# Two transformer blocks on one core: attention weights left undivided until after the values

## The chip, the core and the metric

The kernel runs on one core of a Trainium2 chip, in one launch. The time is that of the device, in microseconds (us), from the start to the end of the program; the median of a few runs is given. PE is the matrix engine, PEld its weight loads, DVE the vector engine, ACT the scalar engine, POOL the general one, SP the queue that issues most transfers. The matrix engine writes into PSUM, eight banks of 128 x 512 float32.

## The reference

512 latent tokens and 256 context tokens of width 1024 go through two blocks of two layers each, batch 1, all in float32.

- Block 1, each layer: a gated linear attention (4 heads), a sliding-window attention (6 query heads over 2 key heads, window 128, all 256 context keys, and a sink) and a neighbourhood attention (6 heads, 8 rows x 32 columns of keys with a learned bias, and the context keys), then an output projection and a SwiGLU. In the first layer the context tokens run through the same steps (there both attentions see the 256 context keys alone).
- Block 2, each layer: an attention over the 128 keys that an indexer selects (8 heads), whose output is normalised per head by its root mean square; an mLSTM beside it; output projection; SwiGLU.

What matters here is the softmax. With a sink it is

```
p = softmax(concat([s_loc, s_ctx, s_sink]))      # the sink is only in the sum
o = p_loc @ v_loc + p_ctx @ v_ctx
```

and without one the same without s_sink. In block 2 the output o then goes through `o * rsqrt(mean(o * o) + 1e-6) * w` per head of 64.

## The kernel before, in words

Activations lie with features on the 128 partitions and tokens along the free axis, weights are loaded in units of 128 x 1024 and split into two parts (`split`, L183), and each product of a projection is three matrix products of these parts (L147, L148, L150). PSUM's eight banks are dealt out as four pools: three for projections (`mm`), two for scores (`S`), two for transposes and broadcasts (`T`), one for attention outputs (`o`).

`attn_pair` (L341) does one block of 128 queries for two heads, whose features are the lower and upper 64 partitions. Scores go to an `S` bank for each head (L365, L369); DVE adds the negated bias or mask on the way to SBUF and keeps the running minimum (L377, two instructions, the second reads the minimum out); ACT takes the exponential with the row's sum (L382); DVE takes the reciprocal of that sum (L383) and multiplies the 128 x 512 or 128 x 640 weights by it (L384); PE transposes them (L392), ACT copies the first head's transposed weights to SBUF (L395), DVE the second's (L397); PE multiplies them with the values (L400) into the pair's `o` bank. For the sink, an extra column of the score buffer holds the negated sink (L357), so that the sum has it. The score buffers `sb` come from a pool of two in the latents' passes, three in the context's pass and four in block 2.

Three callers loop over pairs of heads and blocks of 128 queries. In `mixers` (block 1) they are three pairs of sliding-window heads, then three pairs of neighbourhood heads, each with four blocks for the latents and two for the context; after a pair the output is split from PSUM into two parts for the projection (L187 on ACT, L188 on DVE). In `mixers2` (block 2) the loop is over two halves of the tokens and four pairs, and after each pair the output is squared, normalised by `head_rms` and stored.

Between the blocks the code takes work from a queue of jobs (`tick`): projections of later pairs and output projections, as long as there are any. The Tile framework records all instructions, a list scheduler sets each engine's static order, and pools decide when a buffer comes free: an instruction that writes a buffer waits until the last reader of its former content is done.

Two helpers spread small columns over partitions. `bcast_rows` (L241) gives every partition a row of per-token factors by a matrix product of the broadcast column with the identity (L245), one for each 128 tokens. `head_rms` (L516) does so for the two halves apart (L527), two for each 128 tokens; it is called by the gated linear attention's output (`gla_out`) and by `mixers2`.

Of the kernel before, what the change touches and what calls it, by code (L numbers as in the profile page):

```python
# [10 lines left out]
F32 = mybir.dt.float32  # L11
# [40 lines left out]
class Kern:  # L52
# [90 lines left out]
    def gemm(self, out, terms):  # L143
        """out = the sum over terms (w_hi, w_lo, x_hi, x_lo) of w^T x; the low parts of w come last."""
# [33 lines left out]
    def side_banks(self):  # L178
        """banks that stand idle at the start of a phase"""
# [3 lines left out]
    def split(self, hi, lo, ps, scale=1.0):  # L183
        """hi + lo = scale * ps, hi rounded to float32r."""
# [9 lines left out]
    def rsqrt(self, pool, src, n, eps=EPS):  # L194
        V = self.nc.vector
        x, y, a, p = [self.til(pool, [P, 16], F32, f"rs{c}")[:, :n] for c in "xyap"]
        V.tensor_scalar(x, src, eps, None, op0=ALU.add)
# [13 lines left out]
    def sq_add(self, sg, k, x=None, pe=False):  # L211
        """pe: summed by the tensor engine, where the vector engine has enough to do"""
# [28 lines left out]
    def bcast_rows(self, r, n):  # L241
        """psum[p, 128 j + i] = r[i, j] for all p."""
        ps = self.bank(self.psT, "T")
        for j in range(n // P):
            self.nc.tensor.matmul(ps[:, j * P:(j + 1) * P], r[:, j:j + 1].to_broadcast([P, P]), self.ident, start=True, stop=True)  # L245
# [9 lines left out]
    def norm_seg(self, sg, a, b, h):  # L255
        """h = (x * rms) * a + b in two parts, of one segment."""
# [11 lines left out]
    def mod_units(self, wm, bm, cst, out, chunks, pool=None):  # L268
        """out[:, u, v] for chunks of 4 u; yields after each unit of two k-tiles.
        pool: for the raw weights, where nothing else wants the banks."""  # L270
# [37 lines left out]
    def mod_units_v(self, wm, bm, cv, out, chunks, pool, nv=lambda q: 1):  # L308
        """the same on the vector engine, for nv(q) of the vectors; yields after each unit."""
# [26 lines left out]
    def table(self):  # L336
        """exp and ln from one table set, from here on"""
        self.tc.keep_in_program_order(self.nc.scalar.preload_act_table_set("natural_log_exp_and_others"))

# [1 line left out]
    def attn_pair(self, heads, wide):  # L341
        """heads: dicts of q (hi, lo) or (plain, ), segs (k_hi, k_lo, n) along the keys, bias(c0, w): what is added to
        the negated scores (so that the running extreme is a minimum), init, sink, vs, o."""
# [10 lines left out]
        for x in heads:  # L354
            x["sb"], x["st"] = self.til(self.pb, [P, wide + 1], F32, "sb"), self.til(self.st, [P, 3], F32, "st")
            if x["sink"] is not None:
                V.tensor_copy(x["sb"][:, tot:tot + 1], x["sink"])  # L357
        for bi, (b0, w, idx) in enumerate(banks):
# [12 lines left out]
            for x, ps in zip(heads, pss):  # L371
# [5 lines left out]
                V.tensor_tensor_reduce(dst, src, bt, 1.0, x["init"], ALU.add, ALU.min, x["st"][:, bi:bi + 1])  # L377
                x["init"] = x["st"][:, bi:bi + 1]
        for x in heads:
            st, sb = x["st"], x["sb"][:, :tot]  # L380
            se = x["sb"][:, :tot + (x["sink"] is not None)]
            A.activation(se, se, AF.Exp, bias=x["init"], scale=-1.0, accum_out=st[:, 2:3])  # L382
            V.reciprocal(st[:, 2:3], st[:, 2:3])  # L383
            V.tensor_scalar(sb, sb, st[:, 2:3], None, op0=ALU.mult)  # L384
# [17 lines left out]
    def nat_gemm(self, units, h, toks, n, evac):  # L402
        """out[tok, n cols] for each 128 tokens; units: the k-tiles in equal parts, [P, per * n] each."""
# [75 lines left out]
    def gla_out(self, n, pair, v, dirs, gcol, sg, y):  # L479
        """dirs: per direction (q_in, k_in, states); y: (hi, lo) of [P, n]."""  # L480
# [35 lines left out]
    def head_rms(self, sq, n, rb=None):  # L516
        """1 / rms over each half of the partitions, broadcast back to [P, n] (in psum: rb)."""
# [5 lines left out]
        r = self.rsqrt(self.sm, ms[:, :2 * nt], 2 * nt)  # L523
        rb = self.bank(self.psS, "S") if rb is None else rb
        for j in range(nt):
            for i in range(2):
                nc.tensor.matmul(rb[64 * i:64 * i + 64, j * P:(j + 1) * P], r[:, 2 * j + i:2 * j + i + 1].to_broadcast([P, 64]),  # L527
                                 self.ident, start=True, stop=True)
        return rb

    def out_unit(self, src, u, per, ys, st, gcol, sg=None):
        """x += gcol * (w^T y) for columns [u * per, ...) of one unit [P, len(ys), per], of all tokens or of one segment."""
# [15 lines left out]
    def by_segs(self, segs, units, emit, cont, common=0):  # L548
        """emit(sgs, u): the first units of all segments together, the others segment by segment, and then
# [1253 lines left out]
```

## Time and profile before

| what | value |
|---|---|
| median of three runs | 3463.4 us (3456.02 to 3464.35) |
| profiled execution, its own time from first to last instruction | 3456.8 us |
| PE busy | 3340.1 us, 97%, 21110 instructions |
| DVE busy | 2104.6 us, 61%, 4540 instructions |
| ACT busy | 1322.4 us, 38%, 2322 instructions |
| POOL busy | 34.9 us, 1% |
| mean granted clock of PE | 0.974 |

The five attention stages lie at 115 to 225 us (context, first layer), 366 to 577 and 1330 to 1537 (latents, first and second layer), 2157 to 2275 and 2912 to 3037 (block 2). The busy time of PE contains the modelled tails of its matrix products, so a stretch with PE busy to 95% can still have waits in it; the starts of successive instructions tell more than their durations. "L400" is line 400 of the kernel, and an engine name in front says who executes it. [...]

### The profile page before, as it was taken

The page shows a single profiled execution, that of the slowest core. Times are in us where ns is not written, and L with a number is a line of the kernel's source. Part 1 is how long each engine was busy: PE and PEld are TensorE (multiplying, and loading weights), DVE is VectorE, ACT ScalarE, POOL GpSimd, SP SyncE. Part 2 cuts the span into 40 slices and gives each one's busy share as a digit, 9 for nine tenths or more (in the row PEclk, how much of TensorE's full clock was granted, in tenths as well). Part 3 has the DMA queues.
Part 4 walks back from the last instruction along what each step waited for, and adds up shares of the span by engine and source line. Part 5 has one row for each costly group of instructions (what it writes and reads, how often), then busy time and mean ns, then how long its engine had stood idle before and what let it go on. Part 6 is the DMA issues. An engine that isn't in the chain of part 4 may idle for free.

```text
span 3456.8 us, 53203 instructions
## 1 busy us (share of the span) xinstructions
PE 3340.1 (97%) x21110; PEld 2766.9 (80%) x21110; DVE 2104.6 (61%) x4540; ACT 1322.4 (38%) x2322; POOL 34.9 (1%) x62
## 2 busy tenths in 40 slices
PE   7999999999999999999999999999999999999999
PEld 5777667888889986678889977678889867688889
DVE  4656567645345856667665798565656797463335
ACT  4334244312122543443223474333224474343334
POOL 0000100000000000000000000000000000000000
PEclk9799999999999999999999999999999999899999
DMA  7353212324233421124664411145555211133335
GB/s 258 102 168 102 56 43 68 115 89 130 96 122 122 136 79 48 37 75 150 210 192 158 130 55 61 35 137 171 191 176 170 96 49 62 37 104 98 98 107 164
DMA packets 128768, 388.80 MB, mean 112 GB/s; under 512 B 27268, under 2 KB 32644, under 8 KB 128520
## 3 DMA queue, kind: packets, MB, share of 16 engines
q1 hardware_dynamic: 128520, 385.41, 34.8%
q8 instruction: 166, 2.72, 0.3%
q14 instruction: 82, 0.67, 0.1%
HBM read 383.25 MB, written 2.10 MB: 111 GB/s over the span
## 4 chain that ended last, share of the span: by engine, by line
PE 86%; DVE 7%; ACT 3%; DMA 2%; issue 2%; SPq 0%; DVEq 0%; ACTq 0%
PE mm L147 14%; PE mm L148 13%; PE mm L150 13%; PE mm L141 4%; PE mm L140 4%; PE mm L139 4%; PE o L400 3%; PE S L172 3%; PE mm L1288 3%; PE T L392 2%; PE S L369 2%; DVE wlo L188 1%; PE mm L172 1%; PE o L172 1%; PE S L365 1%
## 5 line engine op out<-in xcount | busy, mean ns | idle before, releaser
L188 DVE TENSOR_TENSOR wlo<-wraw,whi 128x1024 fp32r<-128x1024 f32 (+3 forms) x492 | 575.1, 1173 | 679.1 <-PE mm L150 397.2
L187 ACT CAST whi<-wraw 128x1024 fp32r<-128x1024 f32 (+3 forms) x492 | 494.9, 1010 | 874.4 <-PE mm L148 438.0
L147 PE MATMUL mm<-h_lat,whi 128*128 128x512 f32 x1816 | 722.0, 398 | 0.4 <-ACT whi L187 0.3
L148 PE MATMUL mm<-h_lat,whi 128*128 128x512 f32 x1816 | 716.7, 395 | 0.0
L150 PE MATMUL mm<-h_lat,wlo 128*128 128x512 f32 x1816 | 465.2, 393 | 0.0
L147 PEld LDWEIGHTS mm<-h_lat,whi 128*128 128x128 f32 x1816 | 342.0, 188 | 83.3 <-issue 6.8
L148 PEld LDWEIGHTS mm<-h_lat,whi 128*128 128x128 f32 x1816 | 342.2, 188 | 78.7 <-issue 11.7
L150 PEld LDWEIGHTS mm<-h_lat,wlo 128*128 128x128 f32 x1816 | 337.4, 188 | 75.3 <-issue 5.4
L325 DVE SCALAR_TENSOR_TENSOR macc<-mraw,cst,macc 128x512 f32<-128x512 f32 x280 | 207.1, 749 | 36.3 <-DMA mraw<-wm 32.3
L139 PE MATMUL mm<-ah,whi 128*128 128x256 f32 (+1 forms) x702 | 216.4, 308 | 1.2 <-DVE x_lat L1506 1.2
L140 PE MATMUL mm<-al,whi 128*128 128x256 f32 (+1 forms) x702 | 216.7, 309 | 0.0
L141 PE MATMUL mm<-ah,wlo 128*128 128x256 f32 (+1 forms) x702 | 216.7, 309 | 0.0
L382 ACT ACTIVATE sb<-sb,st 128x512 f32<-128x512 f32 (+6 forms) x184 | 119.7, 651 | 158.6 <-DVE st L377 125.9
L139 PEld LDWEIGHTS mm<-ah,whi 128*128 128x128 f32 x702 | 131.8, 188 | 9.0 <-ACT whi L187 1.4
L141 PEld LDWEIGHTS mm<-ah,wlo 128*128 128x128 f32 x702 | 131.8, 188 | 8.1
L140 PEld LDWEIGHTS mm<-al,whi 128*128 128x128 f32 x702 | 132.2, 188 | 7.4
L140 PE MATMUL mm<-b,whi 128*128 128x256 f32 (+1 forms) x462 | 136.9, 296 | 0.0
L139 PE MATMUL mm<-b,whi 128*128 128x256 f32 (+1 forms) x462 | 136.3, 295 | 0.0
L141 PE MATMUL mm<-b,wlo 128*128 128x256 f32 (+1 forms) x462 | 136.3, 295 | 0.0
L187 ACT CAST ah<-fx 128x256 fp32r<-128x256 f32 (+1 forms) x77 | 43.0, 559 | 199.9 <-DVE fx L876 199.9
L392 PE MATMUL T<-ident,sb 128*128 128x128 f32 x616 | 107.0, 294 | 9.0 <-DVE sb L384 3.6
L392 PEld LDWEIGHTS T<-ident,sb 128*128 128x128 f32 x616 | 73.1, 147 | 43.8 <-issue 16.5
(402 smaller groups left out, 6391.9 us busy)
## 6 DMA issues: line engine op xcount, KB each, us to landing
mraw<-wm SPq DMA_DIRECT2D x144, 512.0 KB
wraw<-wgu SPq DMA_DIRECT2D x88, 512.0 KB
wraw<-wgub SPq DMA_DIRECT2D x88, 512.0 KB
wraw<-wA SPq DMA_DIRECT2D x78, 512.0 KB
wraw<-wB SPq DMA_DIRECT2D x54, 512.0 KB
wraw<-wdb SPq DMA_DIRECT2D x56, 448.0 KB
wraw<-wm SPq DMA_DIRECT2D x48, 512.0 KB
wraw<-wd SPq DMA_DIRECT2D x44, 448.0 KB
```

The costliest lines, as they stand in the source:

```text
L139: mm(out, wh, xh, start=start, stop=False)
L140: mm(out, wh, xl, start=False, stop=False)
L141: mm(out, wl, xh, start=False, stop=stop)
L147: mm(out, wh, xh, start=i == 0, stop=False)
L148: mm(out, wh, xl, start=False, stop=False)
L150: mm(out, wl, xh, start=False, stop=i == len(terms) - 1)
L172: mm(ps[:m, x], w[a][:, c], h[b][:, k, x], start=k == 0 and i == 0, stop=k == KT - 1 and i == 2)
L187: nc.scalar.copy(hi, ps)
L188: nc.vector.tensor_tensor(lo, ps, f32(hi), op=ALU.subtract)
L325: V.scalar_tensor_tensor(acc[v], raw[:, i * 512:(i + 1) * 512], c, acc[v], ALU.mult, ALU.add)
L382: A.activation(se, se, AF.Exp, bias=x["init"], scale=-1.0, accum_out=st[:, 2:3])
L392: T_.transpose(ps[:, j * P:(j + 1) * P], x["sb"][:, (b0 + j) * P:(b0 + j + 1) * P], self.ident)
```

## The change

Comments were taken out as well, so that line numbers differ. What the change does:

- In `attn_pair` the exponentials stay undivided: the reciprocal and the scaling of the weights go, and so does the sink's column. The caller hands in the columns where a row's sum and minimum are kept.
- In `mixers` a new function `over` divides the output of a whole pair once: the reciprocal of all its sums (128 x 8 for four blocks), its broadcast over the two halves of 64 partitions (`bcast_halves`), a copy of that to SBUF (the tile `g`), and one multiplication with the `o` bank. The split then reads `g` instead of `o`. For the sink, exp(minimum - negated sink) is added to the sums, with all its blocks at once.
- In `mixers2` nothing is divided. The norm that follows does not change when o is multiplied by a number, but for its epsilon, so that epsilon is multiplied by the square of the sum (tile `eps`).
- `bcast_halves` copies each factor to 64 columns on ACT (tile `sq`, 128 x 256 for two token tiles) and transposes these with PE, one for each 128 tokens. `head_rms` uses it in place of L527. `bcast_rows` transposes the broadcast column instead of multiplying it with the identity.
- The pool with the score buffers has three instead of two in the latents' passes, four instead of three in the context's.
- The four bias tiles of the neighbourhood attention become one, with one stretch of zeros for the context keys instead of four.

```diff
     def bcast_rows(self, r, n):
         ps = self.bank(self.psT, "T")
         for j in range(n // P):
-            self.nc.tensor.matmul(ps[:, j * P:(j + 1) * P], r[:, j:j + 1].to_broadcast([P, P]), self.ident, start=True, stop=True)
+            self.nc.tensor.transpose(ps[:, j * P:(j + 1) * P], r[:, j:j + 1].to_broadcast([P, P]), self.ident)
+        return ps
+
+    def bcast_halves(self, r, n, ps):
+        for j in range(n // P):
+            if j % 2 == 0:
+                x = self.til(self.sm, [P, SEG], F32, "sq")
+                self.nc.scalar.copy(x.rearrange("p (b o) -> p b o", o=64),
+                                    r[:, 2 * j:2 * j + 4].rearrange("p (b o) -> p b o", o=1).to_broadcast([P, 4, 64]))
+            self.nc.tensor.transpose(ps[:, j * P:(j + 1) * P], x[:, j % 2 * P:(j % 2 + 1) * P], self.ident)
         return ps
...
     def attn_pair(self, heads, wide):
...
-            x["sb"], x["st"] = self.til(self.pb, [P, wide + 1], F32, "sb"), self.til(self.st, [P, 3], F32, "st")
-            if x["sink"] is not None:
-                V.tensor_copy(x["sb"][:, tot:tot + 1], x["sink"])
+            x["sb"], x["st"] = self.til(self.pb, [P, wide], F32, "sb"), self.til(self.st, [P, 2], F32, "st")
...
-                V.tensor_tensor_reduce(dst, src, bt, 1.0, x["init"], ALU.add, ALU.min, x["st"][:, bi:bi + 1])
-                x["init"] = x["st"][:, bi:bi + 1]
+                to = x["least"] if bi == len(banks) - 1 else x["st"][:, bi:bi + 1]
+                V.tensor_tensor_reduce(dst, src, bt, 1.0, x["init"], ALU.add, ALU.min, to)
+                x["init"] = to
         for x in heads:
-            st, sb = x["st"], x["sb"][:, :tot]
-            se = x["sb"][:, :tot + (x["sink"] is not None)]
-            A.activation(se, se, AF.Exp, bias=x["init"], scale=-1.0, accum_out=st[:, 2:3])
-            V.reciprocal(st[:, 2:3], st[:, 2:3])
-            V.tensor_scalar(sb, sb, st[:, 2:3], None, op0=ALU.mult)
+            sb = x["sb"][:, :tot]
+            A.activation(sb, sb, AF.Exp, bias=x["init"], scale=-1.0, accum_out=x["sum"])
...
     def head_rms(...)
-        r = self.rsqrt(self.sm, ms[:, :2 * nt], 2 * nt)
+        r = self.rsqrt(self.sm, ms[:, :2 * nt], 2 * nt, eps)
         rb = self.bank(self.psS, "S") if rb is None else rb
-        for j in range(nt):
-            for i in range(2):
-                nc.tensor.matmul(rb[64 * i:64 * i + 64, j * P:(j + 1) * P], r[:, 2 * j + i:2 * j + i + 1].to_broadcast([P, 64]),
-                                 self.ident, start=True, stop=True)
-        return rb
+        return self.bcast_halves(r, n, rb)
...
     def mixers(...)
-        self.vp, self.pb, ac = apool("vp", 2), apool("pb", 2 if not ctx else 3), apool("ac", 1)
+        self.vp, self.pb, ac = apool("vp", 2), apool("pb", 3 if not ctx else 4), apool("ac", 1)
...
-            self.bias = [self.til(ac, [P, 1024], F32, f"bias{i}") for i in range(4)]
-            for b in self.bias:
-                nc.gpsimd.memset(b[:, 768:1024], 0.0)
+            self.bias = self.til(ac, [P, 4 * 768 + 256], F32, "bias")
+            nc.gpsimd.memset(self.bias[:, 4 * 768:], 0.0)
...
+        pair = lambda s: self.til(self.st, [P, nt, 2], F32, s)
+
+        def over(o, sums):
+            V.reciprocal(sums, sums)
+            x = gt()
+            A.copy(x, self.bcast_halves(sums.rearrange("p b i -> p (b i)"), n, self.bank(self.psT, "T"))[:, :n])
+            V.tensor_tensor(x, x, o[:, :n], op=ALU.mult)
+            return x
...
-            self.split(y[0], y[1], o[:, :n])
+            V.tensor_tensor(least, least, self.nsink[:, p:p + 4:3].rearrange("p (o i) -> p o i", o=1).to_broadcast([P, nt, 2]), op=ALU.subtract)
+            A.activation(least, least, AF.Exp)
+            V.tensor_tensor(sums, sums, least, op=ALU.add)
+            self.split(y[0], y[1], over(o, sums))
...
-            self.split(pv(y[0]), pv(y[1]), pw(o[:, :n]))
+            o = over(o, sums)
+            self.split(pv(y[0]), pv(y[1]), pw(o))
...
     def mixers2(...)
-                self.head_rms(sq, sg.n, rb)
+                e = self.til(self.st, [P, sg.n // P, 2], F32, "eps")
+                V.scalar_tensor_tensor(e, sums, EPS, sums, ALU.mult, ALU.mult)
+                self.head_rms(sq, sg.n, rb, e.rearrange("p b i -> p (b i)"))
```

DVE at the end of the last pair of neighbourhood heads in the second layer (the trace has it at 1520 to 1541); `sb` are score buffers, `st` the minimum and sum, `pt` the transposed weights. Before:

```order
L377 ISA sb_15025,st_15026<-S_15028,bias_13056 128x512
L377 ISA st_15026 128x1
L383 RECIPROCAL st_15024<-st_15024 128x1
L384 TENSOR_SCALAR sb_15023<-sb_15023,st_15024 128x512
L383 RECIPROCAL st_15026<-st_15026 128x1
L384 TENSOR_SCALAR sb_15025<-sb_15025,st_15026 128x512
L377 ISA sb_15071,st_15072<-S_15075,bias_13055 128x512
L377 ISA st_15072 128x1
L397 COPY pt_15056<-T_15057 128x512
```

The same place after, up to the split of the pair's output (`least` and `sums` belong to the pair, `g` is its divided output):

```order
L390 ISA sb_14981,least_14889<-S_14984,bias_13043 128x512
L390 ISA least_14889 128x1
L390 ISA sb_15023,least_14889<-S_15027,bias_13043 128x512
L390 ISA least_14889 128x1
L407 COPY pt_15008<-T_15009 128x512
L390 ISA sb_15025,least_14889<-S_15028,bias_13043 128x512
L390 ISA least_14889 128x1
L769 RECIPROCAL sums_14890<-sums_14890 128x8
L407 COPY pt_15052<-T_15053 128x512
L772 TENSOR_TENSOR g_15070<-g_15070,o_14888 128x512
L188 TENSOR_TENSOR yl_15068<-g_15070,yh_15067 128x8x8x8
```

Between the second head's pass over its scores and the next block's first pass stood four instructions of division, and now none; the pair's reciprocal and product stand at its end.

ACT at the end of that pair, before (`yh` and `yl` are the split output, `whi` a weight):

```order
L382 ACTIVATE sb_15071,st_15072<-sb_15071,st_15072 128x512
L382 ACTIVATE sb_15073,st_15074<-sb_15073,st_15074 128x512
L395 COPY pt_15097<-T_15098 128x512
L187 CAST yh_15119<-o_14926 128x8x8x8
L187 CAST whi_15229<-wraw_15228 128x768
```

and after:

```order
L394 ACTIVATE sb_15023,sums_14890<-sb_15023,least_14889 128x512
L394 ACTIVATE sb_15025,sums_14890<-sb_15025,least_14889 128x512
L405 COPY pt_15045<-T_15046 128x512
L256 COPY sq_15072<-sums_14890 128x256
L256 COPY sq_15076<-sums_14890 128x256
L771 COPY g_15070<-T_15071 128x512
L187 CAST yh_15067<-g_15070 128x8x8x8
L187 CAST whi_15190<-wraw_15189 128x768
```

Three copies have come in between the last copy of transposed weights and the split.

PE at the end of the second layer's last gated linear attention pair, where `head_rms` gets its factors `rsy` from DVE and the first scores of the sliding window follow. Before:

```order
L506 MATMUL o_12926<-gd_12886,gs_12914 64x64 x16
L522 MATMUL S_13003<-sel_310,gd_12999 128x2 x4
L527 MATMUL S_13022<-ident,rsy_13009 64x128 x8
L369 MATMUL S_13190<-qh_12753,qh_12854 128x256
L369 MATMUL S_13190<-qh_12754,qh_12854 128x256
```

and after (`sq` is ACT's copy of the factors):

```order
L516 MATMUL o_12914<-gd_12874,gs_12902 64x64 x16
L532 MATMUL S_12991<-sel_310,gd_12987 128x2 x4
L258 MATMUL S_13010<-ident,sq_13011 128x128 x2
L381 MATMUL S_13172<-qh_12741,qh_12842 128x256
L258 MATMUL S_13010<-ident,sq_13015 128x128 x2
L381 MATMUL S_13172<-qh_12742,qh_12842 128x256
```

Eight products of 64 rows have become four transposes of 128, which read what ACT copied instead of what DVE wrote.

## Rows read from the trace of the kernel before

**Rows 1.** The page: busy us of each engine, then the chain by engine

```profile
PE 3340.1 (97%) x21110; PEld 2766.9 (80%) x21110; DVE 2104.6 (61%) x4540; ACT 1322.4 (38%) x2322; POOL 34.9 (1%) x62
...
PE 86%; DVE 7%; ACT 3%; DMA 2%; issue 2%; SPq 0%; DVEq 0%; ACTq 0%
```

**Rows 2.** Stretches of the attention stages: length, busy us (instructions), PE's clock, DMA

```profile
2157.00:2275.00 118.00, 115.33 (x619) 75.50 (x617) 64.43 (x248) 43.77 (x118) 0.00 (x0) 0.94 0.14 45
2912.00:3037.00 125.00, 122.33 (x624) 78.63 (x623) 64.62 (x248) 44.51 (x121) 0.00 (x0) 0.89 0.13 43
...
sum 771.00, PE 747.86 PEld 530.27 DVE 458.49 ACT 296.15 POOL 28.52; mean PE 149.57 PEld 106.06 DVE 91.70 ACT 59.23 POOL 5.71
```

**Rows 3.** The same view of 445:475, 555:577, 1400:1435 and 1520:1537

```profile
445.00:475.00 30.00, 28.14 (x212) 20.40 (x213) 21.95 (x71) 15.41 (x36) 0.00 (x0) 1.00 0.07 18
...
1520.00:1537.00 17.00, 15.09 (x125) 10.97 (x123) 11.40 (x31) 8.01 (x19) 0.00 (x0) 1.00 0.01 1
sum 104.00, PE 95.79 PEld 69.79 DVE 72.99 ACT 50.23 POOL 0.00; mean PE 23.95 PEld 17.45 DVE 18.25 ACT 12.56 POOL 0.00
```

**Rows 4.** Chain of waits by line, 445:475 and then 1520:1537

```profile
by line: PE S L369 36.3%; PE o L400 24.5%; PE T L392 21.6%; PE mm L147 5.9%; ACT pt L395 4.0%; PE mm L148 3.8%; DVE sb L377 3.2%; issue 1.2%; DVE st L377 0.1%; ACTq L395 0.1%
...
by line: PE S L369 23.3%; PE o L400 23.1%; PE T L392 21.5%; DVE sb L384 8.7%; issue 5.8%; ACT sb L382 4.8%; DVE pt L397 4.3%; DVE sb L377 4.0%; ACT yh L187 3.5%; DVE st L383 2.6%; DVE st L377 0.0%
```

**Rows 5.** Groups: line, xcount, then busy us, mean ns; then idle before

```profile
L245 PE MATMUL T<-ident,rsy 128*128 128x128 f32 x132 | 23.8, 309 | 13.9 <-DVE rsy L207 13.4
L527 PE MATMUL o<-ident,rsy 128*64 128x128 f32 x128 | 11.8, 312 | 0.2
L245 PE MATMUL T<-ident,den 128*128 128x128 f32 x64 | 7.9, 277 | 0.4 <-DVE den L1238 0.4
L527 PE MATMUL S<-ident,rsy 128*64 128x128 f32 x80 | 7.5, 340 | 5.2 <-DVE rsy L207 5.2
...
L384 DVE TENSOR_SCALAR sb<-sb,st 128x512 f32<-128x512 f32 (+4 forms) x184 | 81.6, 446 | 3.9
L383 DVE RECIPROCAL st<-st 128x1 f32<-128x1 f32 x184 | 28.8, 159 | 16.2 <-ACT sb L382 15.4
```

**Rows 6.** Timeline of PE: start, us, what, idle before; broadcasts and what follows

```profile
1328.28 1.58 PE L527 MATMUL S<-ident,rsy 128*64 128x128 f32 x16 [2.16 <-DVE rsy L207]
...
2139.22 2.02 PE L245 MATMUL T<-ident,den 128*128 128x128 f32 x16 [0.22 <-DVE den L1238]
2141.00 0.36 PE L412 MATMUL mm<-whi,h_lat 128*128 128x256 f32 x1
...
2177.03 0.66 PE L527 MATMUL o<-ident,rsy 128*64 128x128 f32 x8
2177.62 0.33 PE L392 MATMUL T<-ident,sb 128*128 128x128 f32 x1
```

**Rows 7.** Timeline of PE in the last pair of the second layer

```profile
1529.34 0.66 PE L392 MATMUL T<-ident,sb 128*128 128x128 f32 x4
1529.92 0.50 PE L369 MATMUL S<-nkc,qh 64*128 64x256 f32 x2
...
1533.09 0.63 PE L392 MATMUL T<-ident,sb 128*128 128x128 f32 x4 [0.21 <-DVE sb L384]
```

**Rows 8.** Timeline of DVE in the same stretch

```profile
1530.03 0.69 DVE L377 CUSTOM_DVE_ANT_0 sb<-S,bias 128x512 f32<-128x512 f32 x1 [0.60 <-PE T L392]
...
1533.28 0.16 DVE L383 RECIPROCAL st<-st 128x1 f32<-128x1 f32 x1 [0.34 <-ACT sb L382]
1533.48 0.49 DVE L384 TENSOR_SCALAR sb<-sb,st 128x512 f32<-128x512 f32 x1
```

**Rows 9.** Groups of ACT, by shape: a copy of 128x256

```profile
L187 ACT CAST ah<-fx 128x256 fp32r<-128x256 f32 x22 | 8.9, 405 | 65.6 <-DVE fx L876 65.6
```

**Rows 10.** Timeline of DVE and of PE at the end of a pair

```profile
1370.59 0.69 DVE L188 TENSOR_TENSOR yl<-o,yh 128x512 fp32r<-128x512 f32 x1
...
1375.08 0.43 PE L400 MATMUL o<-pt,sv 128*64 128x128 f32 x2
```

More of the change, by code (lines that the diff above doesn't have):

```diff
@@ L196, in rsqrt @@
         x, y, a, p = [self.til(pool, [P, 16], F32, f"rs{c}")[:, :n] for c in "xyap"]
-        V.tensor_scalar(x, src, eps, None, op0=ALU.add)
+        if isinstance(eps, float):
+            V.tensor_scalar(x, src, eps, None, op0=ALU.add)
+        else:
+            V.tensor_tensor(x, src, eps, op=ALU.add)
         V.tensor_scalar(y.bitcast(I32), x.bitcast(I32), -0.5, float(0x5F1FFFF9), op0=ALU.mult, op1=ALU.add)
@@ L514, in gla_out, with head_rms @@
         self.split(y[0], y[1], t1)
-    def head_rms(self, sq, n, rb=None):
+    def head_rms(self, sq, n, rb=None, eps=EPS):
         nc = self.nc
@@ L762, in mixers @@
             q = self.need(j_sq[p])
-            o = self.bank(self.pso, "o")
+            o, least, sums = self.bank(self.pso, "o"), pair("least"), pair("sums")
             for b in range(nt):
@@ L788, in mixers @@
                     ns = self.nsink[:, hd:hd + 1]
-                    heads.append(dict(q=(q[0][r, c], q[1][r, c]), segs=segs, bias=bias, init=ns, sink=ns, vs=vs, o=o[r, c]))
+                    heads.append(dict(q=(q[0][r, c], q[1][r, c]), segs=segs, bias=bias, init=ns, vs=vs, o=o[r, c],
+                                      least=least[:, b, i:i + 1], sum=sums[:, b, i:i + 1]))
                 self.attn_pair(heads, 256 if ctx else 640)
@@ L807, in mixers @@
             vv, nk, q = [self.need(j) for j in j_n[p]]
-            o = self.bank(self.pso, "o")
+            o, least, sums = self.bank(self.pso, "o"), pair("least"), pair("sums")
             for b in range(nt):
@@ L825, in mixers @@
                         bt = nb_[2 * p + i]
-                        bias = lambda c0, w, ty=ty, bt=bt: bass.AP(bt.tensor, bt.offset + 256 * ty, [bt.ap[0], [256 * (3 - ty), 2], [1, 256]])
-                    heads.append(dict(q=(q[0][r, c], q[1][r, c]), segs=segs, bias=bias, init=NEG, sink=None, vs=vs, o=o[r, c]))
+                        to = 256 * (12 - ty) - 768 * ((2 * p + i) % 4)
+                        bias = lambda c0, w, ty=ty, bt=bt, to=to: bass.AP(bt.tensor, bt.offset + 256 * ty, [bt.ap[0], [to, 2], [1, 256]])
+                    heads.append(dict(q=(q[0][r, c], q[1][r, c]), segs=segs, bias=bias, init=NEG, vs=vs, o=o[r, c],
+                                      least=least[:, b, i:i + 1], sum=sums[:, b, i:i + 1]))
                 self.attn_pair(heads, 256 if ctx else 640)
@@ L850, in na_bias @@
                 nc.sync.dma_start(raw[mq * 64 + r * 8:mq * 64 + r * 8 + 8], src)
-        bt = self.bias[hd % 4]
+        bt = self.bias[:, 768 * (hd % 4):768 * (hd % 4 + 1)]
         for ty, off in enumerate((16, 8, 0)):
@@ L1295, in mixers2 @@
                 o, rb = o[:, :sg.n], o[:, 256:256 + sg.n]
+                least, sums = [self.til(self.st, [P, sg.n // P, 2], F32, x) for x in ("least", "sums")]
                 for b in range(sg.off // P, (sg.off + sg.n) // P):
@@ L1303, in mixers2 @@
                         bias = (lambda c0, w: self.trineg) if b == 0 else (lambda c0, w, b=b: works[b])
-                        heads.append(dict(q=(q[r, c],), segs=[(k[r, :n], None, n)], bias=bias, init=NEG, sink=None,
+                        j = b - sg.off // P
+                        heads.append(dict(q=(q[r, c],), segs=[(k[r, :n], None, n)], bias=bias, init=NEG,
+                                          least=least[:, j, i:i + 1], sum=sums[:, j, i:i + 1],
                                           vs=[v[:, j, (2 * p + i) * 64:(2 * p + i + 1) * 64] for j in range(b + 1)], o=o[r, oc]))
```

## The prediction

> **What bounds the kernel now.** I read the page's busy shares first, then the stretches of the attention stages, then the chain within them, and last the single instructions. PE is busy 97% of the span, and it makes up 86% of the chain that ended last, where DVE has 7% and ACT 3% [rows 1]. So what counts is an instruction that leaves PE, or a wait that PE stands in. DVE's 61% matters only where PE waits for it.
>
> The change touches five attention stages, 771 us in all, of which PE is busy 747.9 us and DVE 458.5 us; 23.1 us are open idleness of PE [rows 2]. In most of that time projections of later work lie between the attention blocks. Four stretches have little of it: 104 us with PE 95.8 and DVE 73.0 us busy, so 8.2 of the 23.1 us idle lie there, in a seventh of the time [rows 3]. They are where waits inside a block can show.
>
> How much they show is where the views disagree. In 445 to 475 the chain runs through scores, values and transposes, and the scaling on DVE (L384) is not in it at all. In 1520 to 1537 L384 and the reciprocal (L383) have 8.7 + 2.6 = 11.3% of the chain, 1.9 us of 17 [rows 4].
>
> **The change part by part.** The profiled span is 3456.8 us; the median of the three timed runs, 3463.4, lies 6.6 us above it. I sum against the span and add 6.6.
>
> *Broadcasts on PE.* A broadcast by a matrix product is shown as two PE instructions for each 128 columns. L245 has 132 + 64 = 196 of them, for 98 tiles of 128 tokens [rows 5]. Sixteen take 2141.00 − 2139.22 = 1.78 us, 0.111 us each [rows 6], so 21.8 us. As transposes, which the trace shows as one instruction for 128 columns (L392), they become 98. At 0.111 that is 10.9: −10.9 us. L527 has 128 + 80 [rows 5]; eight of them took 2177.62 − 2177.03 = 0.59 us, 0.074 each [rows 6], so 15.4 us. One transpose for four of them gives 52, 5.8 us: −9.6. The divisions add 12 pairs with four token tiles and 6 with two, 60 transposes: +6.7. The sum is −13.8 if a transpose goes at the pitch of L245. Four transposes beside a block's other matrix products take 0.58 us from start to next start, 0.145 each [rows 7]; for 210 of them this adds 210 × 0.034 = 7.1, so −6.7 is the other end. I take −12: most of them follow each other as the sixteen do.
>
> *Reciprocal and scaling leave each head.* 184 × 446 ns and 184 × 159 ns, 81.6 + 28.8 = 110 us of DVE's work [rows 5], go. What PE gains is only what stood on its path. In the last pair of the layer the reciprocal starts at 1533.28, when the exponentials end, and the scaling ends at 1533.97, 0.69 us before which the transposes can't start [rows 8]. There blocks follow each other at 3.75 us (transposes at 1529.34 and 1533.09 [rows 7]). The third score buffer belongs to the same place: at 1530.03 DVE waits 0.60 us for transposes, which is the score buffer that is not yet free [rows 8]. In the new order that pass follows at once on the last pair's second pass, where four instructions stood between.
> Lower end in the four stretches: by the chain nothing in 445 to 475 and 1.9 us in 1520 to 1537; with the other two like these, −4. Upper end: DVE's work in a block is 2 × (0.69 + 0.16 + 0.49) + 0.69, some 3.4 us of the 3.75 by the durations of rows 8 (the copy out of PSUM counted like a pass over the scores). If that sets the pace, a block falls to what PE needs, 15.09 of 17 us or less [rows 3]; 0.75 us of 3.75 gives 104 × 0.20 = −20. I take −10, about the middle: the chain leaves DVE out in one of the two stretches shown, and the waits of rows 8 stand in the other.
> In the other 667 us the open idleness is 23.1 − 8.2 = 14.9 us; projections cover the rest, and weights and the score product's own waits hold part of it. Ends 0 and −15, taken −4.
>
> *What is added.* ACT gets a copy of 128x256 for two token tiles, 0.405 us by the nearest row [rows 9]. In the gated linear attention's norm it stands right between DVE's last step and PE, and PE already waits there (2.16 us before the broadcast at 1328.28 [rows 6]): 6 × (0.4 + some 0.1 of handing over) = +3. In the second block 16 such calls have the output projection's products beside them in the order; between 0 and 16 × 0.5 = 8, taken +1, the cover being those products. For the 18 divisions: one reciprocal, two copies, four transposes, one copy to SBUF, one product of 128x512. All but the product need only the sums, which are there with the exponentials, ahead of the block's last transposes and values; only the product (0.69, as the pass that subtracts, [rows 10]) comes behind the values. At a stage's end it takes the place of a 0.69 us chain that stood ahead of the transposes. In the middle the one o bank is what could be late; today it is free at 1371.28 and wanted at 1375.08, 3.8 us later [rows 10], and now the split reads SBUF, so the bank waits for one pass on o instead of two. Ends: −5 (the bank earlier) and +18 (1 us each where ACT, in order, holds these copies ahead of the next exponentials); taken +2. Sum of the part +6.
>
> *At nothing:* the sink's column (60 small copies become 27 small steps), the shared zeros (POOL 1% busy [rows 1]; each bias slot still waits for its own readers), the table of eps. If a shared zero tied two slots together, a block would wait for POOL; the order shows no such wait. SP issues the same transfers.
>
> *Sum:* −12 − 10 − 4 + 6 = −20; 3456.8 − 20 + 6.6 = 3443.
>
> [...]
> [...]
>
> **The rivals.**
> A. *The waits were never on the path.* The chain of 445 to 475 speaks for it [rows 4]; against it speaks the last pair, where PE's transposes follow the scaling. −12 − 4 + 6 = −10: 3453.
> B. *DVE set the pace.* All upper ends: −14 − 20 − 15 + 3 = −46: 3417. For it speak DVE's 73 of 104 us and the wait for the score buffer; against it, that PE is 92% busy there.
> [...]
> D. *The divisions become the wait.* In-order ACT puts two copies and a copy out ahead of the next block's exponentials, 2 × 0.4 + 0.7 (counted like the pass of rows 10) = 1.5 us, 18 times +27, in place of the +2 taken: 3443 + 27 − 2 = 3468, no change. For it: ACT's exponentials lead the transposes; against it: ACT is busy 50 of 104 us in the four stretches [rows 3].
>
> **How the numbers follow.** The forecast has 0.50, A 0.24, B 0.14, C 0.05, D 0.07. About 0.3%, 10 us, is what a measurement of this kernel tells from no change: 3453 to 3474. The forecast's own range, with each term half way to its bounds, is 3429 to 3455. Faster: nine tenths of the forecast, half of A, all of B: 0.71. Slower: C and a little of D: 0.07. No change: the rest, 0.22. The range reaches to B's upper side and through A and D: 3410 to 3464.
>
> **What would show it.** Right: PE has 404 − 210 = 194 fewer broadcast instructions, DVE 100 us less; blocks near the end of the second layer's attention follow each other at 3.2 to 3.4 us instead of 3.75; the five stages together are some 15 us shorter; transposes wait for the exponentials on ACT instead of for the scaling. Wrong: stages of the same length with PE's idleness put down to ACT (D, or A if the block period stays), a granted clock under 0.9 in the four stretches (C), or a gain outside the attention stages larger than the 22 us of the norms' broadcasts, which nothing here foresees.

## The result and the profile after

The changed kernel takes 3419.7 us (median of four runs, 3418.1 to 3425.9) against 3463.9 us for the kernel before in the same comparison: a ratio of 0.9885, 95% interval 0.9855 to 0.9915 (ratios here and below are of the runs of a comparison, not of the two medians). One execution of all the runs below, of the kernel with the gated linear attention's norm by products, took 5137.5 us at a granted clock of 0.57 and is left out of its median and ratio. The profiled execution spans 3417.5 us against 3456.8. That is 39 us less where 20 were forecast; the time lies in the stated range, near its lower part, and twice as far from the time before as the sum had it.

The page's shares hardly moved [rows 1]; first the busy time of each engine, then the chain by engine, of the changed kernel:

```profile
PE 3296.3 (96%) x20916; PEld 2737.2 (80%) x20916; DVE 2025.2 (59%) x4182; ACT 1346.5 (39%) x2405; POOL 32.1 (1%) x56
...
PE 85%; DVE 8%; ACT 3%; DMA 3%; issue 2%; SPq 0%; DVEq 0%; ACTq 0%
```

PE has 194 instructions fewer, as worked out. DVE is busy 79 us less; the durations of its groups sum to 96 us less, near the 100 forecast, and instructions that overlapped count once in the busy time. Where the time went is seen in the attention stages, measured from the first product of scores to the last with values. The columns are as in rows 2: stretch, length, busy us of PE, PEld, DVE, ACT and POOL with instructions, PE's granted clock. The latents' two stages of the kernel before:

```profile
365.90:576.10 210.20, 205.39 (x1298) 148.07 (x1296) 129.81 (x328) 80.81 (x166) 13.14 (x18) 0.97 0.15 40
1329.80:1536.30 206.50, 201.11 (x1291) 144.79 (x1291) 129.36 (x325) 80.79 (x166) 13.47 (x18) 0.99 0.15 42
```

and of the changed kernel the same two, then block 2's two [rows 2]:

```profile
365.40:570.20 204.80, 202.85 (x1318) 146.40 (x1318) 102.98 (x221) 86.95 (x187) 12.69 (x18) 0.98 0.15 41
1335.20:1539.70 204.50, 202.55 (x1318) 146.34 (x1317) 102.83 (x220) 87.02 (x187) 12.67 (x18) 0.98 0.15 41
...
2158.20:2263.20 105.00, 102.90 (x570) 67.63 (x570) 52.06 (x192) 45.58 (x125) 0.00 (x0) 1.00 0.15 51
2892.90:2998.00 105.10, 103.00 (x571) 67.66 (x570) 52.08 (x192) 45.58 (x125) 0.00 (x0) 1.00 0.15 51
```

The latents gained 5.4 and 2.0 us, although DVE lost 27 us of work in each. Block 2's stages fell from 117.6 and 123.6 to 105.0 and 105.1, 31 of the 39 us, and the last column but two shows a part of the reason: their clock of 0.94 and 0.89 is 1.00 now. The five stages together are 42 us shorter, where some 15 were forecast; what lies between and around them is 2 us longer.

The clock of the kernel before fell at one place in each of these two stages, at 2206 and 2960 us, behind the same instructions. The two windows around the first, and the timelines of PE and then DVE ahead of it (start, us, what, idle before and who ended it):

```profile
2200.00:2206.00 6.00, 4.47 (x21) 2.78 (x20) 5.20 (x27) 2.28 (x10) 0.00 (x0) 1.00 0.01 1
2206.00:2210.00 4.00, 4.00 (x15) 1.72 (x13) 2.25 (x10) 1.78 (x6) 0.00 (x0) 0.50 0.00 0
```

```profile
2201.05 0.50 PE L522 MATMUL o<-sel,g 128*128 128x2 f32 x4
2202.45 0.49 PE L365 MATMUL S<-qh,qh 64*128 64x128 f32 x4 [0.90 <-DVE qh L991]
2203.33 0.98 PE L365 MATMUL S<-qh,qh 64*128 64x256 f32 x4 [0.39 <-DVE st L377]
2204.55 0.91 PE L365 MATMUL S<-qh,qh 64*128 64x384 f32 x2 [0.24 <-DVE st L377]
...
2200.38 0.69 DVE L987 TENSOR_TENSOR g<-T,sinT 128x512 f32<-128x512 f32 x1 [1.80 <-PE T L985]
2200.99 0.68 DVE L989 TENSOR_TENSOR g<-g,cosT 128x512 f32<-128x512 f32 x1
2201.71 0.69 DVE L991 TENSOR_TENSOR qh<-g,g 128x512 f32<-128x512 f32 x1
```

PE waits three times for DVE, which is busy 5.20 of 6 us there. The longest wait, 0.90 us, is for the rotation of the next queries (`qh`): three instructions of DVE behind a product of PE (L985). DVE itself stood idle for 1.80 us until that product, so no division is in this wait. The other two are for the minima; the norm's small steps and the divisions lie among these. Behind the stretch the clock is 0.50, for some 14 us (twice the missing 0.06 of 117.6). The same stretch of the changed kernel:

```profile
2200.00:2206.00 6.00, 5.62 (x29) 3.78 (x29) 4.75 (x22) 2.13 (x9) 0.00 (x0) 1.00 0.00 0
2206.00:2210.00 4.00, 4.00 (x25) 2.05 (x25) 2.92 (x12) 2.90 (x9) 0.00 (x0) 1.00 0.02 4
```

```profile
2199.83 1.89 PE L1309 MATMUL mm<-qh,wraw 128*128 128x256 f32 x8
...
2201.92 0.68 PE L1309 MATMUL mm<-qh,wraw 128*128 128x256 f32 x2
2202.53 0.49 PE L377 MATMUL S<-qh,qh 64*128 64x128 f32 x4
```

PE executes 29 instructions instead of 21, the first wait is gone, and the clock stays. The rotation takes 2.0 us as before, but PE has ten instructions of the output projection (L1309) to execute meanwhile, where it had four (L1288). They are not new: of the twelve that stand near this place in both kernels, eight came ahead of the rotation before, and two do now.

The chain near the end of the second layer's attention, 1523 to 1540, of the changed kernel [rows 4 for the kernel before]:

```profile
by line: PE o L410 32.9%; PE T L402 30.0%; PE S L381 29.0%; issue 3.8%; PE T L258 3.6%; DVE sb L390 0.6%; DVE least L390 0.5%; DVEq L772 0.1%
```

DVE has left it: 1.1% where it had some 20% (L384, L397, L377 and L383). PE fills the place, with transposes for the division among it (L258), and the end of the stage came no sooner for that but by a little.

### The profile page after: what moved, and what is told of

It is laid out like the page before. It is cut to its first block, busy times and chain, and to the rows that moved or that the text cites. A ratio compares the mean times of both kernels' runs of the same rounds, so it can differ in the third digit from the quotient of the medians.

```text
span 3417.5 us, 52436 instructions
## 1 busy us (share of the span) xinstructions
PE 3296.3 (96%) x20916; PEld 2737.2 (80%) x20916; DVE 2025.2 (59%) x4182; ACT 1346.5 (39%) x2405; POOL 32.1 (1%) x56
## 4 chain that ended last, share of the span: by engine, by line
PE 85%; DVE 8%; ACT 3%; DMA 3%; issue 2%; SPq 0%; DVEq 0%; ACTq 0%
PE mm L147 14%; PE mm L148 13%; PE mm L150 13%; PE mm L141 5%; PE mm L140 5%; PE mm L139 5%; PE o L410 3%; PE S L172 3%; PE mm L1309 2%; PE T L402 2%; PE S L381 2%; DVE wlo L188 2%; PE o L172 1%; PE mm L172 1%; PE S L147 1%
## 5 line engine op out<-in xcount | busy, mean ns | idle before, releaser
L338 DVE SCALAR_TENSOR_TENSOR macc<-mraw,cst,macc 128x512 f32<-128x512 f32 x280 | 207.2, 750 | 32.9 <-DMA mraw<-wm 28.7
L394 ACT ACTIVATE sb<-sb,least 128x512 f32<-128x512 f32 (+4 forms) x184 | 119.3, 649 | 154.8 <-DVE least L390 153.2
L172 PE MATMUL S<-h_lat,whi 128*128 128x256 f32 (+1 forms) x448 | 94.3, 300 | 6.7 <-ACT h_lat L277 6.5
```

The costliest lines, as they stand in the source:

```text
L172: mm(ps[:m, x], w[a][:, c], h[b][:, k, x], start=k == 0 and i == 0, stop=k == KT - 1 and i == 2)
L338: V.scalar_tensor_tensor(acc[v], raw[:, i * 512:(i + 1) * 512], c, acc[v], ALU.mult, ALU.add)
L394: A.activation(sb, sb, AF.Exp, bias=x["init"], scale=-1.0, accum_out=x["sum"])
```

## The experiments

Theory 1 was that the clock of block 2 is the larger part, held because PE is no longer thin at one place; theory 2 that the broadcasts' fewer products carry the gain; theory 3 that block 1's waits do. Ratios are to the kernel before, on the same chip in the same comparison.

**Block 2's division alone** (the kernel before with this):

```diff
+            if "sum" in x:
+                A.activation(se, se, AF.Exp, bias=x["init"], scale=-1.0, accum_out=x["sum"])
+                continue
...
+                V.scalar_tensor_tensor(e, sums, EPS, sums, ALU.mult, ALU.mult)
+                self.head_rms(sq, sg.n, rb, e.rearrange("p b i -> p (b i)"))
```

> The kernel before, with the division left out in the second block's attention alone (exponentials undivided, epsilon multiplied by the squared sum); everything else as before. Theory 1 (clock): PE loses its clock at 2206 and 2960 because reciprocals and scalings of DVE hold it back there; without them both stages of block 2 run at a granted clock of 1.00 and last about 108 us instead of 118 and 124: -20 to -28, about 3438. Theory 2 (broadcasts): the clock there hangs on the broadcasts' many small products, which stay: both stages keep their clocks of 0.94 and 0.89, -3 to -6, about 3459. Theory 3 (block 1): the gain lies in block 1, 0 to -3 here.

Measured 3435.1 us, 0.9950 (0.9921 to 0.9979). Its stages of block 2:

```profile
2154.60:2264.40 109.80, 107.38 (x613) 69.32 (x612) 52.49 (x192) 43.12 (x118) 0.00 (x0) 1.00 0.15 49
2902.10:3012.10 110.00, 107.40 (x613) 69.31 (x612) 52.61 (x192) 43.13 (x118) 0.00 (x0) 1.00 0.15 49
```

Full clock, 7.8 and 13.6 us less, as theory 1 had it, though not for its reason: no division stands in the wait for `qh`. The rest of its program is that of the kernel before, and its latents' stages lasted 205.8 and 210.2 us where rows of the kernel before showed 210.2 and 206.5: so much the same code differs between executions with the clock in it.

**The broadcasts alone** (the kernel before with this, and `bcast_halves` as in the change):

```diff
-            self.nc.tensor.matmul(ps[:, j * P:(j + 1) * P], r[:, j:j + 1].to_broadcast([P, P]), self.ident, start=True, stop=True)
+            self.nc.tensor.transpose(ps[:, j * P:(j + 1) * P], r[:, j:j + 1].to_broadcast([P, P]), self.ident)
...
-                nc.tensor.matmul(rb[64 * i:64 * i + 64, j * P:(j + 1) * P], r[:, 2 * j + i:2 * j + i + 1].to_broadcast([P, 64]),
-                                 self.ident, start=True, stop=True)
-        return rb
+        return self.bcast_halves(r, n, rb)
```

> The kernel before with its broadcasts made by transposes (and ACT's copies in the heads' norm), division as before. Theory 1: only fewer PE instructions count, 196 x 0.111 to 98 and 208 x 0.074 to 52 x 0.111, less the copies: -12 to -18, about 3449, and the clocks of block 2's stages stay at 0.94 and 0.89 or near. Theory 2: the clock of these stages rises to 1.00, -35, about 3428. Theory 3: as theory 1.

Measured 3427.9 us, 0.9919 (0.9898 to 0.9940), with this first stage of block 2 (the second is the same to 0.1 us):

```profile
2161.10:2268.30 107.20, 105.24 (x575) 70.23 (x574) 64.04 (x248) 45.94 (x125) 0.00 (x0) 1.00 0.15 50
```

Here theory 2's number came true and theory 1's did not: this part alone, too, keeps the clock, with every division of DVE's in place. So neither part alone is the cause; what they have in common had to be found.

**Block 1's part alone**, block 2 dividing each head, and the broadcasts of all norms and rows by products:

```diff
+            if x.get("divide"):
+                V.reciprocal(x["sum"], x["sum"])
+                V.tensor_scalar(sb, sb, x["sum"], None, op0=ALU.mult)
...
-                self.head_rms(sq, sg.n, rb, e.rearrange("p b i -> p (b i)"))
+                self.head_rms(sq, sg.n, rb)
```

> Block 1's part alone: division once for each head pair, three and four score buffers, one bias tile; block 2 divides each head as before, and the norms' broadcasts stay matrix products. Theory 1: the waits there were mostly hidden, 0 to -8, about 3459. Theory 2: the same, 0 to -8. Theory 3: the latents' and the context's stages carry the gain, -15 to -30, about 3440.

Measured 3467.6 us, 1.0027 (1.0006 to 1.0047): a little slower than before. Block 2's first stage shows the clock lost again (the second is the same):

```profile
2154.40:2271.90 117.50, 114.88 (x616) 75.22 (x616) 64.16 (x248) 43.73 (x118) 0.00 (x0) 0.94 0.14 46
...
364.20:568.00 203.80, 201.85 (x1317) 145.78 (x1316) 103.01 (x221) 87.07 (x187) 12.70 (x18) 0.99 0.15 42
```

Theory 3 fell. The latents' stage is 203.8 us at a clock of 0.99, where the block 2 experiment above, with the old code, has 205.8 at 0.99 and the kernel without block 1's part, below, 207.2 at 0.99: 2 to 3.4 us for the whole stage. The profiled execution is the fastest of ten (3449.1 us); where the others lose time is not known.

**The changed kernel with block 2 divided as before** (the last two lines of that diff alone, and `divide` set there):

> The changed kernel, but block 2 divides each head as before (a reciprocal and a scaling of each head's weights on DVE, the plain epsilon). Theory 1: the clock is lost again in block 2's stages (0.9 to 0.95), 20 to 28 us slower than the changed kernel, about 3444. Theory 2: the clock stays at 1.00, since the broadcasts are still transposes: 2 to 6 slower, about 3424. Theory 3: 0 to 3 slower.

Measured 3428.6 us, 0.9930 (0.9904 to 0.9956). Both stages of block 2 last 107.1 us at a clock of 1.00, 2.1 more than in the changed kernel. By the ratios it is some 16 us slower than that, but the intervals overlap. Theory 1's number for it was wrong, as after the broadcasts' run it had to be.

**The rows' broadcasts alone** (only the first of the two replacements above):

> The kernel before with only the rows' broadcasts (98 of them) as transposes; the heads' norms keep their matrix products, and the division stays. Theory 1 (a thin stretch of PE makes the clock fall, and the broadcast of the heads' norm belongs to it): 98 x 0.111 = -11 for PE, and the clock still falls in block 2's two stages: about -8 to -11, 3449. Rival (fewer products as such keep the clock up): the clock is held there, -25, about 3433.

Measured 3453.3 us, 0.9982 (0.9964 to 1.0001). The clock is lost in both stages:

```profile
2157.60:2284.40 126.80, 124.13 (x617) 79.36 (x616) 64.36 (x248) 43.98 (x118) 0.00 (x0) 0.87 0.13 42
2916.40:3035.20 118.80, 116.26 (x616) 75.73 (x616) 64.19 (x248) 43.85 (x118) 0.00 (x0) 0.93 0.14 45
```

98 PE instructions fewer do nothing for it, and the wait for `qh` stands in both layers as before (0.91 and 0.90 us). Of the broadcasts, then, it takes those of the heads' norm to keep the clock, though in the kernel before their products (L527, at 2206.96) come only behind the fall. This is a second execution of the same stages with the same code, and the loss is 34 and 17 us at half speed instead of 14 and 27 (summed over windows of half a us).

**The kernel before, with more work for PE.** Eight products that nobody reads, in each layer:

```diff
+                if p == 3 and sg.off == 0:
+                    d = self.mmbank()
+                    for j in range(8):
+                        nc.tensor.matmul(d[:, :sg.n], self.ident, ya[j % 2][:, :sg.n], start=True, stop=True)
```

> The kernel before with eight more products of 128x256 (nobody reads them) in each of block 2's layers, ahead of the last head pair of the first half, which push products of the output projection into the stretch where PE is thin. They cost 8 x 0.215 us in each layer, +3.4 in all. If that thin stretch (2200 to 2206, PE busy 4.4 of 6 us) is why the clock falls at 2206 and 2960: the stages keep a clock of 1.00 and last some 113 us instead of 118 and 124, about -14 in all, 3445, though work is added. If the clock falls for another reason: +3, and the clocks stay at 0.94 and 0.89.

Measured 3449.0 us, 0.9968 (0.9956 to 0.9980). The stretch that corresponds to 2200 to 2206 (its scores start at 2196.71 instead of 2202.45), and then its two stages:

```profile
2194.30:2200.30 6.00, 5.84 (x31) 3.63 (x31) 5.25 (x27) 2.12 (x9) 0.00 (x0) 1.00 0.00 1
...
2151.10:2265.40 114.30, 112.60 (x632) 74.42 (x632) 64.77 (x248) 43.55 (x118) 0.00 (x0) 1.00 0.15 47
2902.20:3016.60 114.40, 112.69 (x633) 74.51 (x632) 64.81 (x248) 43.57 (x118) 0.00 (x0) 1.00 0.15 47
```

DVE is as busy as before (5.25 of 6 us), all divisions and broadcasts are in place, and PE has 3.4 us more to do. Yet the clock holds and the kernel is 11 us faster. The products pushed some of the output projection's into the stretch, where PE now has 31 instructions instead of 21 and no wait for `qh`. It also gives a price: if its products cost their whole 1.7 us, a stage at full clock would last 112.6 us without them, so the kernel before lost 117.6 − 112.6 = 5.0 and 123.6 − 112.7 = 10.9 us to the clock. Taken between the two layers of one kernel, which needs no such reference, it is a little higher: 6.0 us more for 13.6 us more at half speed, so 0.44 for each, or 6.0 and 12.0 us.

**The changed kernel, made thin at that place.** Four multiplications by one on DVE, which the scores of the last pair wait for:

```diff
+                if p == 3 and sg.off == 0:
+                    for _ in range(4):
+                        V.tensor_scalar(q, q, 1.0, None, op0=ALU.mult)
```

> The changed kernel with four multiplications by one of 128x512 on DVE (0.49 us each) in each of block 2's layers, in the queries of the last head pair of the first half, which PE's scores there wait for: PE becomes thin again where the kernel before lost its clock. The work itself delays PE by 2.0 us at most in each layer, +4. [...] If the clock of that place hung on the divisions or on the broadcasts' products themselves: the clock stays at 1.00, +4 or less, 3423.

Measured 3440.7 us, 0.9936 (0.9920 to 0.9953), some 18 us more than the changed kernel by the ratios (the profiled execution is the slowest of four, 3445.3 us). PE's wait, the windows around it and the two stages:

```profile
2202.52 0.49 PE L377 MATMUL S<-qh,qh 64*128 64x128 f32 x4 [1.50 <-DVE qh L1320]
```

```profile
2199.00:2203.10 4.10, 2.51 (x16) 1.78 (x14) 3.76 (x15) 0.00 (x0) 0.00 (x0) 1.00 0.00 0
2203.10:2209.00 5.90, 5.61 (x14) 2.78 (x14) 2.83 (x16) 3.20 (x12) 0.00 (x0) 0.50 0.00 0
...
2156.60:2269.60 113.00, 109.50 (x570) 69.90 (x570) 53.92 (x196) 45.91 (x125) 0.00 (x0) 0.95 0.14 47
2901.20:3025.10 123.90, 120.42 (x570) 74.96 (x570) 54.04 (x196) 45.88 (x125) 0.00 (x0) 0.86 0.13 43
```

With no division and no product of the old broadcasts in block 2, a wait of 1.50 us in that place brings the half clock back: +8.0 and +18.8 us for 2 us of DVE's work in each layer. Together with the run before, this shows it from both sides: with no wait for these queries the clock there stayed at 1.00, and with one of 1.50 us it fell to 0.50. PE's waits for these queries, in total, times and longest, in the kernel before and in this one:

```profile
PE S L365 <- DVE qh L991: 1.8, 2, 0.9
...
PE S L377 <- DVE qh L1320: 3.0, 2, 1.5
```

Block 1's part alone and the rows' broadcasts alone have 1.8 us in two waits there too, and lose the clock in both layers. The changed kernel and the broadcasts alone have none, and their clock is 1.00 in both; so is that of block 2's division alone, of the filled kernel above, of the changed kernel with block 2 divided and of all but block 1's part. The two shorter waits did not take the clock where they stood without the first; the broadcasts alone, with 1.00 throughout, have them still, 0.38 and 0.24 us:

```profile
2204.73 0.68 PE L1293 MATMUL mm<-qh,wraw 128*128 128x256 f32 x2
2205.34 0.49 PE L374 MATMUL S<-qh,qh 64*128 64x128 f32 x4
2206.21 0.98 PE L374 MATMUL S<-qh,qh 64*128 64x256 f32 x4 [0.38 <-DVE st L386]
2207.43 0.91 PE L374 MATMUL S<-qh,qh 64*128 64x384 f32 x2 [0.24 <-DVE st L386]
```

So what block 2's division and the broadcasts have in common is the order of PE's instructions: with the division gone or the heads' norm broadcast by transposes, the scheduler leaves ten or eight of the output projection's twelve to the time of the rotation instead of four. Why it does is not shown.

**All but block 1's part** (broadcasts by transposes and block 2 undivided; block 1's attention, buffers and bias as before):

> The broadcasts by transposes and block 2 undivided, but block 1's attention as before (each head's weights divided, two and three score buffers, four bias tiles). If block 1's part is worth what its latents' stages show, some 2.3 us each at an equal clock: the stages of block 2 last 105 us at a clock of 1.00, the latents' stages as before, 3 to 6 slower than the changed kernel, ratio to the kernel before 0.989 to 0.991, about 3424. If its part costs more elsewhere than it saves, as its run alone (1.0027) has it: 5 to 10 faster than the changed kernel, ratio 0.986 to 0.988, about 3412.

Measured 3424.9 us, 0.9891 (0.9861 to 0.9921), against 0.9885 (0.9855 to 0.9915): not to be told from the changed kernel. Block 2's stages are 105.0 us each, and the latents' first:

```profile
369.10:576.30 207.20, 202.40 (x1298) 146.04 (x1298) 130.00 (x328) 80.82 (x166) 13.14 (x18) 0.99 0.14 41
```

**The score buffers.** The changed kernel with two and three again:

```diff
-        self.vp, self.pb, ac = apool("vp", 2), apool("pb", 3 if not ctx else 4), apool("ac", 1)
+        self.vp, self.pb, ac = apool("vp", 2), apool("pb", 2 if not ctx else 3), apool("ac", 1)
```

> The changed kernel with two (latents) and three (context) score buffers, as before. If the third buffer carries a gain of the latents' stages: each of the two some 3 us longer than in the changed kernel, +6, about 3426. If the gain there comes from the division alone: 0 to +2, about 3421.

Measured 3427.1 us, 0.9904 (0.9884 to 0.9923). The interval overlaps the changed kernel's, and the profiled execution has a mean clock of 0.978 where the changed kernel's has 0.980. Whether the third buffer is worth anything stays open; the ratios differ by some 7 us, within their intervals.

**The gated linear attention's norm by products**, no copy of ACT's between DVE and PE:

```diff
-        rb = self.head_rms(sq, n)
+        rb = self.head_rms(sq, n, mm=True)
```

> The changed kernel, but the gated linear attention's six norms broadcast by matrix products as before, without ACT's copy between DVE and PE. By the prediction's prices (1.07 or 0.53 us less of products each, 0.5 us more for the copy) it is +2, about 3422. If the copy costs more than the products it saves (PE waits 8.2 us for it in three places where it waited 5.2 before): -2 to -5, about 3416.

Measured 3422.7 us (median of three runs), 0.9894 (0.9866 to 0.9922): no difference from the changed kernel that can be told, and so no verdict between the two prices.

**The changed kernel, filled at three more places.** The clock also falls right after PE waits 3.16, 2.51 and 2.51 us for ACT's copy in the second pair of each gated linear attention. In the changed kernel, the timeline and the windows of the context's:

```profile
116.02 0.69 PE L258 MATMUL S<-ident,sq 128*128 128x128 f32 x2 [3.16 <-ACT sq L256]
```

```profile
112.00:116.00 4.00, 0.86 (x6) 0.66 (x6) 3.08 (x12) 1.48 (x3) 0.00 (x0) 0.99 0.64 235
116.00:120.00 4.00, 3.98 (x16) 3.43 (x17) 3.49 (x11) 3.12 (x10) 0.00 (x0) 0.50 0.35 135
```

```diff
+        if idle:
+            d = self.mmbank()
+            for _ in range(idle):
+                nc.tensor.matmul(d[:, :SEG], self.ident, sq[:, :SEG], start=True, stop=True)
```

> The changed kernel with 14 (context) or 11 (latents) products of 128x256 that nobody reads, behind the head norm's sums of the second pair of each gated linear attention, where PE waits 3.2, 2.5 and 2.5 us for ACT's copy and the clock falls right after (116 to 140, 365 to 372, 1334 to 1341). [...] If the clock falls there for another reason, or the products only push other work back: 0 to +6, about 3423.

Measured 3454.7 us, 0.9984 (0.9973 to 0.9994): 34 us slower than the changed kernel, far outside the 0 to +6 expected. The added products made the scheduler order other work anew; the largest of PE's waits is now one that had 4.0 us in the changed kernel:

```profile
PE T L468 <- DVE gd L454: 28.5, 10, 10.9
```

(us in total, times, longest). So this run tells nothing about those three places, and a version faster than the changed kernel was not found.

## Why the prediction was half right

*Direction and range.* Faster, in the range, by twice the sum. The number of rival B (3417) was nearly met, but not for its reason: that was DVE setting the pace in all the attention, and where it was said to, nothing much came.

*The step that failed* is the treatment of the clock. The prediction's own rows show 0.94 and 0.89 in block 2's stages [rows 2], and no term of its sum is for that. It never asked why the clock was low there already, and whether the change touches the place where it fell. It does, though only through the order of PE's instructions: the fall follows a wait of 0.90 us for the rotated queries, in which neither a division nor a broadcast of the norm stands, and either part of the change moves the output projection's instructions into it. No term of the sum is about that order, and that it came out well is luck. Had the sum held the 5.0 + 10.9 us, it would have read −36.

*Its sums.* In rival B the added part goes in as +3, where its own ends give 3 + 0 − 5 = −2; with that B reads −51 and 3412. The range with each term half way to its bounds reaches 3462 by the ends given, not 3455. And the −10 of the four stretches is more than the 8.2 us for which rows 3 have PE idle in them; its upper end of 0.75 us for a block has no row, as PE's 15.09 of 17 us leave 0.42.

*The broadcasts*, taken at −12. In block 2 the stage at full clock goes from 112.6 us (with the filling products taken off) to 107.2 with the broadcasts alone, and from 109.8 to 105.0 on top of the division: 5 us a stage, 0.6 for each of eight calls, where the prediction had 0.59 − 2 × 0.111 = 0.37 less a copy at 0.06. So the copy is covered, as said. Over the whole program the broadcasts alone gained 28 us by their ratio; less the 16 of the clock that is 12, the size of the term. Groups of PE by line, of the changed kernel, with instructions, busy us, mean ns, then idle before [rows 5]:

```profile
L248 PE MATMUL T<-ident,rsy 128*128 128x128 f32 x66 | 14.6, 312 | 13.2 <-DVE rsy L210 12.4
L258 PE MATMUL T<-ident,sq 128*128 128x128 f32 x60 | 10.7, 287 | 0.2
L258 PE MATMUL o<-ident,sq 128*128 128x128 f32 x32 | 6.9, 298 | 0.6 <-ACT sq L256 0.4
L258 PE MATMUL S<-ident,sq 128*128 128x128 f32 x20 | 5.0, 356 | 8.2 <-ACT sq L256 8.2
L248 PE MATMUL T<-ident,den 128*128 128x128 f32 x32 | 4.5, 274 | 0.5 <-DVE den L1259 0.5
```

The counts are 98 and 112, as worked out; the last but one shows the wait for ACT's copy in the gated linear attention, 8.2 us where 5.2 stood: +3, as taken. The part of the 0.6 us that the 0.37 does not explain was not pursued.

*The division.* Block 2, in the "other 667 us" taken at −4: measured 112.6 − 109.8 = 2.8 us a stage, 2.1 on top of the broadcasts, so 4 to 6. Block 1's four stretches and the buffer, taken at −10: the latents' stages show 2 to 3.4 us each at an equal clock, and the kernel without block 1's part is as fast, as far as can be told. Rival A was near there. The chain of 445 to 475, which had no scaling in it, was the better witness than the waits of the last pair: once DVE is out of the chain, PE has 95% of it, and the transposes of the division come on top. Block ends of the last pair were to follow each other at 3.2 to 3.4 us; the last products of the last four blocks lie 11.4 us apart, 3.8 for a block (3.3, 4.9 and 3.1), where they lay 12.4 apart.

*The divisions as a wait* (rival D) did not show: the o bank, the divisions' copies and the sums are nowhere among PE's waits of more than 0.5 us, in total. Only the last pair's split at the ends of the three stages of block 1 is waited for longer, 3.8 us in all (1.5 at most) where it was 2.0.

*A clock under 0.9 in the four stretches* (C) did not come: 445 to 475, 555 to 577, 1400 to 1435 and 1520 to 1537 of the changed kernel have granted clocks of 1.00, 0.92, 1.00 and 1.00. At 1523 to 1540, where the transposes of the weights are 30.0% of the chain, it is 1.00.

*What stays.* Of the 39 us, some 16 are the clock in block 2's stages and 15 the work there (7.6 for each), or 18 and 13 by the price between the layers; the remaining 8 are spread over the other stages and what lies between them, with the clock of each execution in them, and were not settled further.

## What to carry to other kernels

Where a stage shows a granted clock under 1.00, look for the place where it falls and read the few microseconds ahead of it: here a wait of 0.90 us stood ahead of 14 and 27 us at half speed, 5.0 and 10.9 us lost, and changes elsewhere that moved the order of the engine's instructions gave them back. Look, too, for work that could stand in the wait. Price such a wait by the stretch at half speed, not by its own length. And where two views disagree on whether a step stands on the path, weigh the one that holds for more of the time: DVE lost 27 us of work in each latents' stage and the stage lost two to five.

## What was not expected of the hardware

Useless work made the kernel faster: 3.4 us of products that nobody reads saved 11 us, as PE's granted clock then stayed at 1.00 in block 2's stages, where it had been 0.94 and 0.89. Three waits of 0.90, 0.39 and 0.24 us within 3 us were all that PE stood still before it was lost, and without the first of them it was kept. It came back only 14 and 27 us later in the kernel before, although PE was busy in all of that time, and 34 and 17 us later with the rows' broadcasts: how long differed between the two layers and between executions. A us at a granted clock of 0.50 cost 0.36 to 0.47 us in the kernel before and that with the rows' broadcasts (5.0 of 14, 10.9 of 27; between two layers 6.0 of 13.6 and 8.0 of 17).
